# Down projection of an encoder layer: two column halves with kept operands, and seven half-block products with operands made step by step

## The chip, the cores and the metric

The kernel runs on one core of a Trainium2 chip. The metric is the device time of one execution in microseconds (us). A core has five engines that run side by side and meet through semaphores: TensorE (PE, with its weight loads listed as PEld), VectorE (DVE), ScalarE (ACT), GpSimd (POOL) and SyncE (SP), which issues nearly all DMAs here. Each engine takes its instructions in a fixed order that is laid out when the kernel is built.

## The reference

One encoder layer on 1024 tokens of width 1024, float32: a mixer, a cross attention and a gated feed-forward block, each followed by a layer norm of `alpha * h + f(h)`. The change touches the last block alone:

```
def conv_ffn(x, w_up, b_up, w_dw, b_dw, w_down, b_down):
    h = x @ w_up + b_up
    h = depthwise conv of width 3 over positions (h, w_dw) + b_dw
    g, u = jnp.split(h, 2, axis=-1)
    y = jax.nn.gelu(g, approximate=False) * u
    return y @ w_down + b_down

h = layer_norm(ALPHA * h + conv_ffn(h, ...), ln3_w, ln3_b)
```

`y` is 1024 tokens x 2816 features, `w_down` 2816 x 1024.

## The kernel before

**Arithmetic.** Float32 products are made from float16 pairs. An operand is scaled by a power of two and split (`split16`, L204 and L205): ACT writes `hi`, DVE writes `lo = scaled - hi`. `mm3` (L225 to L227) then issues three matmuls, hi x hi, hi x lo and lo x hi. The scale of an operand comes from the largest sum of absolute values of its rows (`scale_of`, L183 to L189): a small matmul `mx` spreads the maxima over the partitions and a few one-column DVE operations make the power of two.

**Up projection.** The loop `for v in range(NFF)` runs over 22 units of 128 gate and 128 value columns. It makes 2x2 blocks of each unit with seven products in place of eight (names `A11 B11` to `A22 T4`); a product is 12 matmuls of 128x512. POOL makes sums of the unit's blocks (L1505 to L1508), ACT and DVE split them two units ahead, ACT and DVE take the products out of PSUM (`take`), and `post(v)` (L1586 to L1594) runs the convolution, the GELU and the product with the value half, stores `y_d[v]` to DRAM with one DMA, and sums the absolute values of `y` for its scale. `survey_down` reads `w_down` for its scale. Unit v's last two products run in iteration v + 1.

**Down projection.** For the first 20 feature blocks the scale of `y` is taken in the last unit (`y_scale(0)`), and another for the last two blocks later (`y_scale(1)`, with `ratio` between the two). `y_pair` loads two blocks of `y` into the `ur` buffers and splits them; the 22 split blocks stay in SBUF and serve both column halves. `w_pair` loads and splits a column half of four blocks of `w_down`. `dmm` adds a list of blocks into one PSUM bank. The first column half runs over five groups of four blocks with eight token tiles in eight banks; the last unit's two remaining products stand in its first group. DVE copies the sums to `half0`. The second half goes tile by tile: POOL makes the residual `r * rw + rb` (L1795, L1796) of a tile of `h2_d`, DVE adds `half0` (L1798) and the PSUM sums (L1801, L1803), then `ln_tile` (L238 to L257) normalises the row, with one POOL operation for the power and one for the bias, and SP stores it.

**Order.** SP, POOL and the other engines take their work in the order that the builder lays out from the program's order and its own estimate of readiness. Buffers are handed on when their last reader is done: `wraw` has two, `whi` and `wlo` five each, `ur` two.

## Time and profile before

| | us |
|---|---|
| runs, median of 3 | 1548.47 (1541.97 to 1549.49) |
| the profiled execution, time | 1548.25 |
| its span, first to last instruction | 1546.5 |
| PE busy in the span | 1471.3 (95%) |
| DVE busy | 1053.5 (68%) |
| ACT busy | 811.2 (52%) |
| POOL busy | 573.3 (37%) |
| mean granted TensorE clock | 0.983 |

The profile is one execution recorded by the hardware profiler. A row of a group reads: line, engine, operation, output<-input tiles, shape, count | busy us in all, mean ns of one | idle time of the engine just before them, and what ended most of it. A row of a timeline reads: start, duration, engine, line, operation, tiles, count, and in brackets the idle time before it and what ended it; neighbours of one line are joined ("x2"), and then the duration runs over both. Matmuls overlap, so a matmul's duration (0.38) is longer than the distance between two starts.

### The profile page before, as it was taken

The page shows a single profiled execution, that of the slowest core. Times are in us where ns is not written, and L with a number is a line of the kernel's source. Part 1 is how long each engine was busy: PE and PEld are TensorE (multiplying, and loading weights), DVE is VectorE, ACT ScalarE, POOL GpSimd, SP SyncE. Part 2 cuts the span into 40 slices and gives each one's busy share as a digit, 9 for nine tenths or more (in the row PEclk, how much of TensorE's full clock was granted, in tenths as well). Part 3 has the DMA queues.
Part 4 walks back from the last instruction along what each step waited for, and adds up shares of the span by engine and source line. Part 5 has one row for each costly group of instructions (what it writes and reads, how often), then busy time and mean ns, then how long its engine had stood idle before and what let it go on. Part 6 is the DMA issues. An engine that isn't in the chain of part 4 may idle for free.

```text
span 1546.5 us, 21750 instructions
## 1 busy us (share of the span) xinstructions
PE 1471.3 (95%) x8134; PEld 877.8 (57%) x8134; DVE 1053.5 (68%) x1961; ACT 811.2 (52%) x1369; POOL 573.3 (37%) x446
## 2 busy tenths in 40 slices
PE   8899899999999899999999997999999999999997
PEld 6788787456765788874455443444444444444443
DVE  7875857535767778575357678888888777947333
ACT  5434475665553576423244676777777765722000
POOL 6243265412334766134112274444444420112252
PEclk9999999999999999999999999999999999999999
DMA  8843554314644742643001333222222433842111
GB/s 297 311 157 127 187 190 168 102 48 113 164 153 146 226 137 82 245 169 145 28 28 55 126 126 120 110 109 109 109 109 109 161 125 101 308 150 82 46 64 55
DMA packets 84896, 208.62 MB, mean 135 GB/s; under 512 B 7091, under 2 KB 36019, under 8 KB 81462
## 3 DMA queue, kind: packets, MB, share of 16 engines
q1 hardware_dynamic: 84496, 206.46, 38.3%
q8 instruction: 64, 1.05, 0.3%
q0 software_dynamic: 144, 0.49, 0.2%
q14 instruction: 42, 0.34, 0.1%
q10 hardware_dynamic: 150, 0.27, 0.0%
HBM read 158.34 MB, written 49.35 MB: 134 GB/s over the span
## 4 chain that ended last, share of the span: by engine, by line
PE 57%; DVE 21%; DMA 8%; ACT 8%; issue 4%; SPq 1%; POOL 1%; DVEq 0%; ACTq 0%; POOLq 0%
PE dn L226 5%; PE dn L227 5%; PE dn L225 5%; PE S L225 4%; PE S L227 4%; PE S L226 4%; DMA sv<-in_w_down_dram 3%; DVE cbuf L1587 3%; DVE cbuf L1588 3%; DVE wlo L205 2%; PE cl L225 2%; PE tk L225 2%; PE cl L227 2%; PE cl L226 2%; PE tk L227 2%
## 5 line engine op out<-in xcount | busy, mean ns | idle before, releaser
L1505 POOL TENSOR_TENSOR wraw<-ur 128x512 f32<-128x512 f32 x22 | 43.2, 1963 | 197.6 <-issue 189.4
L226 PE MATMUL dn<-wlo,yp 128*128 128x512 f16 x272 | 103.3, 382 | 2.7 <-DVE wlo L205 2.7
L1587 DVE SCALAR_TENSOR_TENSOR cbuf<-C,wdw,cbuf 128x1024 f32<-128x1024 f32 x44 | 79.9, 1818 | 35.7 <-ACT cbuf L1586 35.7
L227 PE MATMUL dn<-whi,yp 128*128 128x512 f16 x272 | 103.5, 382 | 0.0
L225 PE MATMUL dn<-whi,yp 128*128 128x512 f16 x272 | 102.9, 382 | 0.5 <-ACT whi L204 0.5
L226 PEld LDWEIGHTS <-whi 128*128 128x128 f16 x540 | 53.3, 99 | 61.8 <-issue 9.4
L227 PEld LDWEIGHTS <-wlo 128*128 128x128 f16 x540 | 53.4, 99 | 61.2 <-DVE wlo L205 5.3
L225 PEld LDWEIGHTS <-whi 128*128 128x128 f16 x540 | 53.2, 99 | 55.5 <-ACT whi L204 2.1
L253 ACT ACTIVATE r<-r,lnrs 128x1024 f32<-128x1024 f32 x19 | 23.6, 1243 | 114.5 <-DVE lnrs L252 114.5
L205 DVE SCALAR_TENSOR_TENSOR wlo<-wraw,us,whi 128x1024 f16<-128x1024 f32 (+1 forms) x48 | 65.5, 1381 | 23.6 <-ACT whi L204 23.3
L1588 DVE SCALAR_TENSOR_TENSOR cbuf<-C,wdw,cbuf 128x1024 f32<-128x1024 f32 x44 | 72.0, 1637 | 1.3
L243 POOL TENSOR_TENSOR lnrs<-lnrs,mhalf 128x1 f32<-128x1 f32 x32 | 18.8, 590 | 115.0 <-DVE lnrs L242 99.4
L227 PEld LDWEIGHTS <-yp 128*128 128x128 f16 x352 | 34.5, 98 | 44.9 <-issue 3.8
L1586 ACT ACTIVATE cbuf<-C,bdw,wdw 128x1024 f32<-128x1024 f32 x44 | 54.3, 1237 | 10.5 <-DVE C L1623 9.8
L225 PE MATMUL tk<-whi,Be 128*128 128x256 f16 (+1 forms) x192 | 54.8, 286 | 4.6 <-DVE stage L205 3.3
L225 PEld LDWEIGHTS <-yp 128*128 128x128 f16 x352 | 34.5, 98 | 42.6 <-issue 1.4
L226 PEld LDWEIGHTS <-yp 128*128 128x128 f16 x352 | 34.6, 98 | 41.9 <-issue 0.8
L204 ACT ACTIVATE whi<-wraw,us 128x1024 f16<-128x1024 f32 (+1 forms) x48 | 51.2, 1103 | 13.1 <-DVE us L177 11.1
L225 PE MATMUL tk<-whi,Bo 128*128 128x256 f16 (+1 forms) x192 | 52.9, 275 | 2.4 <-DVE gm L399 2.4
L226 PE MATMUL tk<-wlo,Be 128*128 128x256 f16 (+1 forms) x192 | 54.5, 285 | 0.0
L227 PE MATMUL tk<-whi,Be 128*128 128x256 f16 (+1 forms) x192 | 54.5, 284 | 0.0
L1182 ACT ACTIVATE P<-P,mn 128x256 f32<-128x256 f32 (+1 forms) x64 | 35.7, 558 | 34.0 <-DVE mn L1180 33.8
(502 smaller groups left out, 4941.4 us busy)
## 6 DMA issues: line engine op xcount, KB each, us to landing
ur<-in_w_up_dram SPq DMA_DIRECT2D x22, 1024.0 KB
sv<-in_w_down_dram SPq DMA_DIRECT2D x22, 512.0 KB
y<-cbuf SPq DMA_DIRECT2D x22, 512.0 KB
ur<-y SPq DMA_DIRECT2D x11, 1024.0 KB
wraw<-in_w_down_dram SPq DMA_DIRECT2D x22, 512.0 KB
r<-h SPq DMA_DIRECT2D x19, 512.0 KB
h<-r SPq DMA_DIRECT2D x16, 512.0 KB
wraw<-in_w_tok_dram SPq DMA_DIRECT2D x10, 512.0 KB
```

The lines of the kernel that those rows point to most:

```text
L204: A.activation(hi, src, AF.Copy, scale=s)
L205: return V.scalar_tensor_tensor(lo, src, s, hi, op0=OP.mult, op1=OP.subtract)
L225: T.matmul(ps, lh, rh, start=first, stop=False, skip_group_check=skip)
L226: T.matmul(ps, lh, rl, start=False, stop=False, skip_group_check=skip)
L227: return T.matmul(ps, ll, rh, start=False, stop=last, skip_group_check=skip)
L243: G.tensor_tensor(rs[:, 0:1], rs[:, 0:1], mhalf[:, 0:1], OP.pow)
L253: A.activation(r, r, AF.Identity, scale=rs[:, 0:1], bias=rs[:, 1:2])
L1182: A.activation(P[:, :nk], P[:, :nk], AF.Exp, scale=-1.0, bias=mn[:, 0:1], accum_out=mn[:, 1:2])
L1505: G.tensor_tensor(S1, A21, A22, OP.add)
L1586: A.activation(c, C[:, 1:SEQ + 1], AF.Identity, scale=wdw[:, 1, j:j + 1], bias=bdw[:, j:j + 1])
L1587: V.scalar_tensor_tensor(c, C[:, 0:SEQ], wdw[:, 0, j:j + 1], c, op0=OP.mult, op1=OP.add)
L1588: V.scalar_tensor_tensor(c, C[:, 2:SEQ + 2], wdw[:, 2, j:j + 1], c, op0=OP.mult, op1=OP.add)
```

## The change

The down projection is cut into 2x2 blocks: features 0 to 1407 and 1408 to 2815 (11 blocks of 128 each, `NH`), output columns 0 to 511 and 512 to 1023, and even and odd token tiles. It is computed as seven products (`order`), each over 11 steps and four token tiles in four PSUM banks. A step is one feature block: one operand of 128x512 from `y` and one of 128x512 from `w_down`.

- `load_step` loads the parts of a step, `prep_step` makes its sums and differences on POOL and DVE and splits them, `step` issues its 12 matmuls (three for each of four tiles). `ahead` keeps splits 6 steps (first product) or 10 steps ahead of the matmuls and loads 10 or 13 ahead. Thirteen buffers hold split operands, five hold loaded parts; the blocks A and B of the first product and the sums S and T stay in pages.
- The eleven steps of the first product are loaded in the last unit but one and the first six split in the last unit, with a scale from the first half of `y`; all other products use a scale from all of `y`, known after the last `post`. `ratio` brings the first product to it.
- `y_d[v]` is stored with two DMAs, even and odd token tiles apart, in runs of 512 bytes.
- `residual` computes `h2 * rw + rb` on POOL in every second unit and stores it in `res_d`; at the end `rows` loads it and ACT multiplies it by the scale.
- After each product its four banks are added to `M`, `U` or the rows, on ACT, DVE and POOL. The even tiles are normalised after the fifth product, with the weight multiplied on POOL (`weng`); the odd ones in the last product, which runs two tiles over all steps, then the third, then the fourth.

```diff
+            def residual(tt):
...
+                S.dma_start(r, h2_d[tt * 128:(tt + 1) * 128, :])
+                G.tensor_tensor(r, r, rw, OP.mult)
+                G.tensor_tensor(r, r, rb, OP.add)
+                S.dma_start(res_d[tt * 128:(tt + 1) * 128, :], r)
+            order = ("A11 B11", "S1 T1", "S2 T2", "A12 B21", "S4 B22", "S3 T3", "A22 T4")
+            steps = [(n, j) for n in order for j in range(NH)]
+            def load_step(i):
...
+                if i % 5 < 2:
+                    t = wp.tile([128, WP], F32, name="wraw", tag="wraw", bufs=2)[:, :1024]
                 else:
+                    t = page["pool"].tile([128, 1024], F32, name="tm", tag="tm", bufs=3)
...
+                S.dma_start(t0, y_part(h, a, j))
+                if n == "S1 T1":
+                    S.dma_start(page["S"][j], y_part(0, 1, j))
+                    S.dma_start(page["T"][j], w_part(0, 1, j))
+                elif n != "S4 B22":
+                    S.dma_start(t1, w_part(n != "S3 T3", n == "S3 T3", j))
+            def prep_step(i):
...
+                elif n == "S1 T1":
+                    G.tensor_tensor(page["S"][j], page["S"][j], y, OP.add)
+                    V.tensor_tensor(page["T"][j], page["T"][j], B_, OP.subtract)
+                    y, w = page["S"][j], page["T"][j]
+                elif n == "S2 T2":
+                    y, w = page["S"][j], page["T"][j]
+                    G.tensor_tensor(y, y, A_, OP.subtract)
+                    V.tensor_tensor(w, B_, w, OP.subtract)
+                elif n == "S4 B22":
+                    G.tensor_tensor(y, y, page["S"][j], OP.subtract)
+                    w = B_
+                elif n == "S3 T3":
+                    G.tensor_tensor(y, A_, y, OP.subtract)
+                    V.tensor_tensor(w, B_, w, OP.subtract)
+                elif n == "A22 T4":
+                    G.tensor_tensor(w, w, page["T"][j], OP.subtract)
...
+                split16(o[0], o[1], y, sc_y[i >= NH])
+                split16(o[2], o[3], w, sd)
+            def step(ps, i, qs):
+                j = i % NH
+                yh, yl, wh, wl = ops[i]
+                for q in qs:
+                    c = slice(q * 128, q * 128 + 128)
+                    mm3(ps[q], yh[:, c], yl[:, c], wh, wl, j == 0, j == NH - 1)
...
+            for m in range(7):
...
+                if m == 6:
+                    for j in range(NH):
+                        ahead(i0 + j, 10, 13)
+                        step(ps, i0 + j, (0, 1))
+                    for q in range(4):
+                        if q > 1:
+                            for j in range(NH):
+                                step(ps, i0 + j, (q,))
+                        r0, r1, r = odd[q]
+                        add(V, r0, ps[q])
+                        finish(r, 2 * q + 1, late=q == 3)
+                    break
+                for j in range(4 if m == 0 else 0, NH):
+                    ahead(i0 + j, 10 if m else 6, 13 if m else 10)
+                    step(ps, i0 + j, range(4))
+                    if (m, j) == (1, 0):
+                        even = rows("X2l", 0)
+                    if (m, j) == (5, 3):
+                        odd = rows("X1h", 1)
+                        for q in range(4):
+                            add(G, odd[q][1], U[q])
+                for q in range(4):
+                    if m == 0:
+                        A.activation(M[q], ps[q], AF.Copy, scale=ratio)
+                    if m == 1:
+                        A.activation(U[q], ps[q], AF.Copy)
+                        add(G, even[q][0], M[q])
+                    if m == 2:
+                        add(V, M[q], ps[q])
+                        add(G, U[q], M[q])
+                        add(G, even[q][1], U[q])
+                    if m == 3:
+                        add(V, even[q][0], ps[q])
+                    if m == 4:
+                        add(V, even[q][1], ps[q])
+                        finish(even[q][2], 2 * q, weng=G)
+                    if m == 5:
+                        add(V, M[q], ps[q])
+                        add(V, odd[q][1], ps[q])
+                        add(G, odd[q][0], M[q])
```

More of the change, by code (lines that the diff above doesn't have):

```diff
@@ L1667, in dmm @@
-            def dmm(ps, tt, c, fs, first, last):
-                t0 = slice(tt * 128, tt * 128 + 128)
-                for f in fs:
-                    wh, wl = wdn[c, f // 4]
-                    mm3(ps, ys[f][0][:, t0], ys[f][1][:, t0], wh[:, f % 4, :], wl[:, f % 4, :],
-                        first and f == fs[0], last and f == fs[-1])
-            sy = {}
-            def y_scale(g):
-                sy[g] = scale_of(ysum[:, :NG] if g == 0 else ysum[:, NG:], 14)
+            rw, rb = vec(2, "ln2_w"), wk.tile([128, D], F32, name="rb")
@@ new lines, in prep_step @@
+            def prep_step(i):
+                n, j = steps[i]
+                A_, B_ = page["A"][j], page["B"][j]
+                y, w = temps.pop(i, (None, None))
+                if n == "A11 B11":
+                    y, w = A_, B_
+                elif n == "S1 T1":
[14 more added lines that the diff above has]
+                    G.tensor_tensor(w, w, page["T"][j], OP.subtract)
+                k = i % 13 if i >= NH else i % 2 * 5
+                if k < 10:
+                    t = wp.tile([128, 2048], F16, name=("whi", "wlo")[k // 5], tag=("whi", "wlo")[k // 5], bufs=5)
+                else:
+                    t = page["pool"].tile([128, 2048], F16, name="op", tag="op", bufs=3)
+                o = ops[i] = [t[:, q * 512:q * 512 + 512] for q in range(4)]
+                split16(o[0], o[1], y, sc_y[i >= NH])
+                split16(o[2], o[3], w, sd)
@@ new lines, in ahead @@
+            def ahead(i, preps, loads):
+                while at[0] < len(steps) and (at[0] <= i + loads or at[1] + 1 > at[0]):
+                    load_step(at[0])
+                    at[0] += 1
+                while at[1] < len(steps) and at[1] <= i + preps:
+                    prep_step(at[1])
+                    at[1] += 1
+            def step(ps, i, qs):
[4 more added lines that the diff above has]
+                    mm3(ps[q], yh[:, c], yl[:, c], wh, wl, j == 0, j == NH - 1)
@@ L1706, in encoder @@
                 if v == NFF - 1:
[L1707 removed]
+                    for i in range(2, 4):
+                        prep_step(i)
                 if v > 0:
```

212 lines of the change are left out of this document (96 added, 116 removed).

## The prediction

> **What bounds the kernel now.** I read the page first, then the stage table over the end of the run, then the chain of waits, then the timelines of single engines around the clashes. In the stage table the columns after the stretch are its length and the busy time and count of PE, PEld, DVE, ACT and POOL, then the granted clock, the DMA share and GB/s.
>
> ```profile
> span 1546.5 us, 21750 instructions
> PE 1471.3 (95%) x8134; PEld 877.8 (57%) x8134; DVE 1053.5 (68%) x1961; ACT 811.2 (52%) x1369; POOL 573.3 (37%) x446
> ```
> ```profile
> 940.00:960.00 20.00, 14.68 (x60) 6.18 (x58) 17.36 (x18) 14.24 (x17) 7.83 (x4) 0.85 0.27 105
> 1000.00:1060.00 60.00, 60.00 (x282) 27.29 (x281) 50.30 (x54) 45.13 (x52) 27.98 (x15) 1.00 0.34 130
> 1300.00:1330.00 30.00, 26.73 (x116) 11.65 (x115) 26.89 (x24) 21.60 (x22) 0.00 (x0) 0.94 0.80 275
> 1360.00:1390.00 30.00, 30.00 (x141) 13.58 (x139) 9.29 (x8) 5.74 (x5) 0.00 (x0) 1.00 0.48 166
> ```
>
> The up projection (1000 to 1060) and the down projection (1360 to 1390) keep PE full. In the down projection DVE and POOL have much idle time; between 940 and 960 and at 1300 PE starves. The PE timeline and the end of the chain of waits give the edges of the stage that changes:
>
> ```profile
> 1294.83 0.38 PE L225 MATMUL z<-TX1h,whi 128*128 128x512 f16 x1
> 1299.79 0.38 PE L227 MATMUL z<-TX1l,wlo 128*128 128x512 f16 x1
> 1304.90 0.38 PE L226 MATMUL dn<-wlo,yp 128*128 128x512 f16 x1 [2.73 <-DVE wlo L205]
> ```
> ```profile
> 1538.56 0.23 PE dn L227
> 1538.81 0.70 DVE wraw L1803
> ```
>
> The first two rows are the ends of 24 matmuls in a row: 4.96 / 23 = 0.2157 us each. The last up product in the main loop ends at 1300.0 (call it T); the first `dn` work then waits for its operands. The last matmul ends at 1538.8, so the stage takes T + 238.8. After it come 7.7 us of tail, which the change keeps.
>
> **PE's share of the change.** Before: 22 blocks x 8 token tiles x 2 column halves x 3 = 1056 matmuls. After: 7 products x 11 steps x 4 tiles x 3 = 924. One step is 12 x 0.2157 = 2.59 us, a product 28.5, all seven 199.3; the 24 matmuls left of the last up unit take 5.2. With nothing late PE would end at T + 204.5, 34.3 us earlier, and the scales, which are now known one unit earlier, also take away the wait after T. The start of the stage is probably that good: the first six operand pairs are 12 `lo` operations, about 8 us of DVE in the last unit, where units are no longer prepared.
>
> **What the operands cost.** Before, an operand was made once and used for many products. After, each of 66 later steps (products 2 to 7) makes two fresh operands of 128x512: ACT writes `hi`, DVE writes `lo`; 33 steps also subtract on DVE, and 55 add or subtract on POOL. No row has DVE's or ACT's split at 512, so I go by nearby rows.
>
> ```profile
> L205 DVE SCALAR_TENSOR_TENSOR wlo<-wraw,us,whi 128x1024 f16<-128x1024 f32 x15 | 18.6, 1279 | 0.0
> L205 DVE SCALAR_TENSOR_TENSOR unitYh<-ur,us,unitYh 128x1536 f16<-128x1536 f32 x4 | 7.3, 1819 | 7.4 <-ACT unitYh L204 7.4
> L204 ACT ACTIVATE whi<-wraw,us 128x1024 f16<-128x1024 f32 x14 | 15.2, 1134 | 0.0
> L1803 DVE TENSOR_TENSOR r<-r,dn 128x512 f32<-128x512 f32 x4 | 2.8, 688 | 23.0 <-PE dn L227 23.0
> L238 DVE BATCH_NORM_STATS2 lnst<-r 128x6 f32<-128x512 f32 x8 | 5.5, 688 | 0.1
> ```
> ```profile
> 1255.03 0.74 DVE L1619 SCALAR_TENSOR_TENSOR C<-z,us,C 128x512 f32<-128x512 f32 x1
> 1255.69 0.74 DVE L1613 SCALAR_TENSOR_TENSOR C<-z,us,C 128x512 f32<-128x512 f32 x1
> ```
>
> `lo`: 1.82 - 1.28 = 0.54 us per 512 columns, so 0.74 alone, and back to back one per 0.66 (the two starts). A DVE add or subtract: one per about 0.62. ACT is below 0.75 each, under 1.5 us of 2.59 per step, so ACT is no bound. DVE by itself takes 2 x 0.66 + 0.62 = 1.94 per step: it would fit.
>
> It doesn't stay by itself. These are POOL alone, then POOL and DVE together, in the two engines' timelines:
>
> ```profile
> 1117.89 1.27 POOL L1508 TENSOR_TENSOR wraw<-ur,wraw 128x512 f32<-128x512 f32 x1
> 1454.03 2.35 POOL L1795 TENSOR_TENSOR r<-r,vec 128x1024 f32<-128x1024 f32 x1 [6.66 <-DMA r<-h]
> ```
> ```profile
> 1111.19 2.19 POOL L1505 TENSOR_TENSOR wraw<-ur 128x512 f32<-128x512 f32 x1 [10.58 <-issue]
> 1113.35 2.25 POOL L1507 TENSOR_TENSOR wraw<-ur 128x512 f32<-128x512 f32 x1
> 1115.56 2.25 POOL L1506 TENSOR_TENSOR wraw<-wraw,ur 128x512 f32<-128x512 f32 x1
> 1346.19 6.61 POOL L1795 TENSOR_TENSOR r<-r,vec 128x1024 f32<-128x1024 f32 x2 [95.95 <-DMA r<-h]
> 1352.76 6.63 POOL L1796 TENSOR_TENSOR r<-r,vec 128x1024 f32<-128x1024 f32 x2
> ```
> ```profile
> 1112.17 2.30 DVE L1587 SCALAR_TENSOR_TENSOR cbuf<-C,wdw,cbuf 128x1024 f32<-128x1024 f32 x1
> 1350.57 6.61 DVE L205 SCALAR_TENSOR_TENSOR wlo<-wraw,sc,whi 128x1024 f16<-128x1024 f32 x2
> 1418.24 0.74 DVE L1777 SCALAR_TENSOR_TENSOR half<-dn,sc,half 128x512 f32<-128x512 f32 x1
> ```
>
> While POOL runs 128x1024, a DVE `lo` of 1024 takes 3.3 us (6.61 / 2) and so does POOL's add: they take turns. One turn of both is 3.3, against 1.2 for DVE alone, so DVE loses 2.1 per POOL operation of 1024, and 2.21 - 1.2 = 1.0 per one of 512 (POOL's starts are 2.21 apart). DVE's work on PSUM isn't held up: L1777 keeps 0.74 beside POOL's 2.36 us add that starts at 1418.28. Before, this clash touched a few rows; after, nearly every step has one.
>
> The page "SBUF — State Buffer" of the Trainium skill (section "SBUF: two separate sides") says that GpSimd and a DVE operation with two SBUF inputs hold their common port pair exclusively, for a whole instruction each. The turns above agree. Were it only a sharing of bandwidth, POOL could lie beside DVE and PE might end at T + 204.5; by the rule the floor worked out below, T + 226, can't be beaten.
>
> **The sum for DVE**, from the moment the common scale is known until the last operand. That scale now needs the last `post`: 10.4 us of the first four steps + 5.2 + a take of 0.74, then L1586, two STT, GELU, product and sum at 1.0 to 1.3 each for one half with the other half's STT between, about 11, and 1 for the scale: T + 28.
> - own work: 132 `lo` x 0.66 = 87.1; 33 subtractions x 0.62 = 20.5; 12 PSUM adds x 0.66 = 7.9; statistics of four even tiles, 1.9 each = 7.5. Sum 123.
> - POOL in the way: 55 operand operations + 16 adds at the ends of products = 71 x 1.0; 8 of 1024 in the even tiles' layer norm x 2.1. Sum 87.8, of which about 10 fall beside the 15.4 us of PSUM adds and statistics: 78.
> - less 5 for the sums of three steps that can be done before the scale: 196.
>
> The last operand is ready at T + 224, where PE wanted it at T + 189. After it PE has one step of two tiles and two tiles of 11 steps: 72 matmuls, 15.5. End T + 239.5, against T + 238.8: **PE's 34 us are given back**, nearly all in the last three products, since products 2 and 3 need 32 us each for PE's 28.5, products 4 and 5 win that back (14 and 26), and then the layer norm of the even tiles lies ahead of the last operands on POOL's queue.
>
> Bounds. Floor: if every gap is filled, the two engines' turns alone are 165 x 0.58 (1.1 per 1024, halved, plus a little) + 71 x 1.13 + 8 x 2.2 = 193.5; five steps' sums done early take 8.6 off: 185 + 26 + 15.5 = T + 226.5, 12 faster. Ceiling: nothing of POOL's 98 hidden, 123 + 98 + 30 + 15.5 = T + 266, 27 slower.
>
> **Waits added.** DVE's L252 waits for POOL's power, with the next operands queued behind it:
>
> ```profile
> L252 DVE TENSOR_SCALAR lnrs<-lnmv,lnrs 128x1 f32<-128x1 f32 x7 | 1.5, 212 | 12.8 <-POOL lnrs L243 12.7
> ```
>
> Four waits of 12.7 / 4 = 3.2 us stood there at no cost; now four stand in DVE's path, 0 to 13 us. I take 4, since other operands are put between. On SP the step loads (132 of 256 KB from product 2 on, 44 in product 2 alone) pass one queue, in which the stores of even tiles wait for POOL; loads run 13 steps ahead, so I cost it at nothing.
>
> ```profile
> 1.26 0.42 SPq L576 DMA_DIRECT2D memraw<-in_memT_dram  x1
> 1.73 0.44 SPq L566 DMA_DIRECT2D wr<-in_w_xk_dram  x1
> 1316.81 1.74 SPq L1662 DMA_DIRECT2D wraw<-in_w_down_dram  x2
> ```
> ```profile
> GB/s 426 401 426 418 393 426 410 418 442 410 385 389 397 389 385 279 168 16 0 49 41 270 418 418 418 434 90 49 139 377 401 418 393 377 377 410 402 401 389 373
> ```
>
> At 0.47 us apart, 44 issues take 21 us; at the 1.2 of the last SP row, 53, and product 2 would be 13 late: that is in the upper end. The bytes of product 2, 11.5 MB at about 400 GB/s (stretch 1325 to 1345), take 29. The page "SBUF — State Buffer" (section "A bandwidth-pool intuition that's wrong") gives 358 GB/s for HBM to core; by that they would take 32, still no more than DVE needs there. The row, 400 and more, decides.
>
> **In the up projection** the residual adds 16 POOL operations of 1024 in units 2 to 16, its loads and stores, and two DVE operations (2 us) in unit 0, near the stretch 940 to 960 where PE already starves. DVE has 9.7 of 60 us free at 1000 to 1060 (3 per unit); two POOL operations per two units take up to 4.2 of 6. Bounds 0 and 10 (2 + half a us each); I take 3. `y` goes out in two stores of 512-byte runs; DMA is 0.34 busy there, so nothing. What is removed with it, POOL's 16 operations and loads at the end, was beside PE and saves nothing there.
>
> **Forecast.** 1548.25 (profiled execution: span 1546.5 plus 1.75) + 0.7 + 4 + 3 = 1556. The median of the runs, 1548.47, is the same within 0.3.
>
> **Rivals.**
> 1. PE stays the bound, or nearly: POOL's layer norm slips behind the last operands (16.8 less) and the clashes fall beside other DVE work. For: the order of a queue is laid out at build time, and in the up projection L1587 is stretched only in part of its runs. Against: the two-turn sum of 193.5 in PE's 161 us (T + 28 to T + 189). Full cover gives 1514, the slipped layer norm 1539: 1514 to 1540.
> 2. Slower by much: the layer norm of the even tiles sits on POOL and makes DVE wait with operands behind it. Price: L252's 13 instead of 4, plus nothing of POOL hidden there (+10), or SP's 1.2 spacing (+13): 1567 to 1590. It decides once DVE has no lead left at product 5's end. Page "TensorE: Matmul & The Clock Gate" of the Trainium skill (Part 1) says that an idle window of about 3.4 us halves PE's clock; the row 940 to 960, with 5.3 us idle and clock 0.85, agrees, and by that a long gap would cost another 2 us.
> 3. The gain is swallowed exactly: turns without gaps, 1536 to 1545.
>
> **Chances.** Forecast, 1545 to 1567, 0.50, half of it on each side of 1556; rival 1 0.22; rival 2 0.18; rival 3 0.10, under half of it faster. A measurement tells 0.5% (7.7 us) from no change: faster 0.26, same 0.31, slower 0.43. The range leaves out rival 1's lower half and rival 2's last third: 1528 to 1583; the likeliest case's own is 1545 to 1567.
>
> **What would show it.** Right: PE idle about 30 us in products 5 to 7, ended by DVE `lo` or ACT `hi`; DVE and POOL together near full from T + 28; `lo` rows of 512 at 0.74 mixed with 1.7 to 1.9 beside POOL; the wait after T gone. Wrong: PE full to the end (rival 1; then the turns weren't the bound), or a PE gap in product 2 released by DMA (SP's spacing), or an up projection longer by over 6 us. The forecast falls if POOL's operations mostly run while DVE waits for something else.

## The result: 1590 us, slower by 2.8%

The changed kernel takes 1590.17 us (median of 5 runs, 1585.76 to 1594.57). The kernel before took 1545.89 us beside it (5 runs, 1541.97 to 1549.49). The ratio is 1.028, with a 95% interval of 1.0249 to 1.031. The forecast was 1556 with a range up to 1583, so the time lies outside the range, on the slower side.

The profiled execution of the changed kernel took 1585.76 us. The first two lines of its page:

```profile
span 1584.0 us, 22134 instructions
...
PE 1461.7 (92%) x8002; PEld 871.3 (55%) x8002; DVE 1172.3 (74%) x2082; ACT 875.7 (55%) x1495; POOL 714.7 (45%) x525
```

The span is 37.5 us longer than before's 1546.5, with 132 matmuls fewer (8002 for 8134). To see where the 37.5 us lie, the run is cut at the same two points as in the prediction: T, the end of the last up product in the main loop, and the last matmul. The PE timeline of the changed kernel:

```profile
1304.86 0.38 PE L226 MATMUL dn<-whi 128*128 128x512 f16 x1
...
1320.83 0.38 PE L228 MATMUL dn<-whi 128*128 128x512 f16 x1
...
1331.19 0.38 PE L228 MATMUL z<-TX1l,wlo 128*128 128x512 f16 x1
...
1572.34 0.38 PE L228 MATMUL dn<-op 128*128 128x512 f16 x1
```

The last `z` of the main loop ends at 1331.4, but 27 matmuls of the down projection (5.8 us; the first two rows are the first and the last of them) had already been pulled in ahead of it, in three runs of 7, 8 and 12. They belong to the later stage, so T is counted as 1325.6 here, against 1300.0 before. The last matmul ends at 1572.7.

| part of the span | before | after | difference | forecast |
|---|---|---|---|---|
| start to T | 1300.0 | 1325.6 | +25.6 | +3 |
| T to the end of the last matmul | 238.8 | 247.1 | +8.3 | +4.7 |
| after the last matmul | 7.7 | 11.3 | +3.6 | 0 |
| span | 1546.5 | 1584.0 | +37.5 | +7.7 |

The stage that was rewritten came out 3.6 us above the forecast, and the tail after it another 3.6. The main loss lies in the up projection, where only the residual, the split store of `y` and the first loads and splits of the new stage were added. One stretch of both kernels in the stage table (columns as in the prediction), before and then after:

```profile
860.00:1300.00 440.00, 420.67 (x1942) 189.81 (x1940) 346.44 (x416) 316.38 (x377) 174.27 (x102) 0.98 0.31 114
```
```profile
860.00:1300.00 440.00, 398.13 (x1809) 177.45 (x1808) 341.11 (x400) 301.64 (x361) 220.16 (x118) 0.98 0.39 134
```

PE got through 133 matmuls fewer in the same 440 us. At 0.2157 us each that is 28.7 us. Up to 860 the changed kernel had issued 15 more than the kernel before (5127 for 5112, by the same view), so at 1300 it is 118 behind, 25.5 us: the whole of T's delay. POOL has 16 operations more (118 for 102) and 46 us more of busy time. DVE is idle for 99 us in this stretch and still seems to have room. This count of matmuls between 860 and 1300 is used below for every run.

The stage rows of the changed kernel that answer to those quoted before:

```profile
940.00:960.00 20.00, 14.20 (x60) 5.93 (x59) 19.91 (x14) 11.16 (x14) 17.77 (x8) 0.93 0.53 184
1000.00:1060.00 60.00, 51.06 (x227) 22.08 (x226) 48.48 (x49) 36.94 (x44) 34.83 (x16) 0.97 0.36 123
...
1360.00:1390.00 30.00, 21.47 (x80) 8.86 (x81) 28.83 (x30) 26.20 (x41) 24.49 (x16) 0.83 0.71 250
1390.00:1420.00 30.00, 25.07 (x104) 10.58 (x102) 30.00 (x34) 15.54 (x25) 12.56 (x8) 0.89 0.00 1
1420.00:1510.00 90.00, 90.00 (x419) 40.83 (x417) 84.02 (x86) 44.25 (x63) 56.56 (x36) 1.00 0.53 169
1510.00:1540.00 30.00, 24.72 (x108) 10.62 (x106) 29.53 (x39) 16.32 (x22) 23.98 (x16) 0.94 0.50 154
1540.00:1584.00 44.00, 24.11 (x89) 9.57 (x88) 34.94 (x45) 4.34 (x4) 30.71 (x18) 0.77 0.23 96
```

Between 1000 and 1060, where PE was full before (282 matmuls), it now issues 227. In the down projection DVE is full (28.83 and 30.00 of 30) while PE has 80 and 104 matmuls in 30 us where 139 would fit: 20 us are lost at the start of product 2, the wait for the common scale with them. Products 3 to 6 (1420 to 1510) run full. Product 7 loses another 20: 197 matmuls from 1510 to the last one's end at 1572.7, where 290 would fit.

The timeline of ACT, DVE, POOL and PE in the changed kernel at those two places:

```profile
1354.10 1.06 ACT L1592 ACTIVATE cbuf<-cbuf 128x1024 f32<-128x1024 f32 x1 [6.61 <-DVE cbuf L1589]
...
1359.63 0.69 DVE L1704 TENSOR_TENSOR pgX2h<-ur,pgX2h 128x512 f32<-128x512 f32 x1 [5.56 <-DMA ur<-in_w_down_dram]
1360.24 1.22 DVE L1593 TENSOR_TENSOR cbuf<-cbuf 128x1024 f32<-128x1024 f32 x1
...
1391.95 1.75 DVE L206 SCALAR_TENSOR_TENSOR op<-pgX1l,sc,op 128x512 f16<-128x512 f32 x1
1393.12 5.05 POOL L1846 TENSOR_TENSOR rows<-rows,half 128x512 f32<-128x512 f32 x3
...
1399.30 0.74 DVE L206 SCALAR_TENSOR_TENSOR op<-pgX1l,sc,op 128x512 f16<-128x512 f32 x1
...
1400.76 1.46 PE L228 MATMUL dn<-wlo 128*128 128x512 f16 x3 [4.93 <-DVE wlo L206]
...
1532.09 13.22 DVE L206 SCALAR_TENSOR_TENSOR wlo<-tm,sc,wlo 128x512 f16<-128x512 f32 x6
...
1533.12 2.79 POOL L257 TENSOR_TENSOR rows<-rows,lw 128x1024 f32<-128x1024 f32 x1
...
1545.22 9.00 DVE L206 SCALAR_TENSOR_TENSOR op<-wraw,sc,op 128x512 f16<-128x512 f32 x4
...
1547.47 5.54 POOL L258 TENSOR_TENSOR rows<-rows,pgX2h 128x1024 f32<-128x1024 f32 x2
1550.86 0.59 PE L227 MATMUL dn<-op 128*128 128x512 f16 x1 [4.01 <-DVE op L206]
...
1554.28 0.58 PE L227 MATMUL dn<-op 128*128 128x512 f16 x1 [0.70 <-DVE op L206]
```

A `lo` of 512 takes 0.74 alone and 1.75 beside a POOL operation of 512; beside POOL's layer norm (1024) and its operand sums (512) six of them take 13.22, 2.2 each. From 1359 on PE's waits end with a `lo`, but for two: 3.57 us for the common scale and 1.76 for ACT's first `hi` after it.

The first three rows show why the scale is late. GELU of the last `post` (L1592) is done at 1355.16, but its product on DVE (L1593) starts only at 1360.24: a difference for product 3 (L1704) stands ahead of it on DVE's queue and waits 5.56 us for its load of `w_down`. SP had issued that load late, after 3.9 us of waiting for a buffer that POOL had to hand back. So 5 us of the scale's delay come from a load; what they cost in the end was not tried.

The residual's POOL operations in the up projection, as the view of the tile `res` lists them (count: least/median/most in ns, first and last start):

```profile
L1647 POOL TENSOR_TENSOR res<-res,vec x8: 2338/2838/3982, 913.1 to 1022.6; 128x1024 f32<-128x1024 f32 x8
L1648 POOL TENSOR_TENSOR res<-res,rb x8: 3211/3222/3350, 918.1 to 1025.0; 128x1024 f32<-128x1024 f32 x8
```

Written into every second unit, they all stand between 913 and 1028 us: the builder took them as early as their loads allowed.

### The profile page after: what moved, and what is told of

It is laid out like the page before. It is cut to its first block, busy times and chain, and to the rows that moved or that the text cites. A ratio compares the mean times of both kernels' runs of the same rounds, so it can differ in the third digit from the quotient of the medians.

```text
span 1584.0 us, 22134 instructions
## 1 busy us (share of the span) xinstructions
PE 1461.7 (92%) x8002; PEld 871.3 (55%) x8002; DVE 1172.3 (74%) x2082; ACT 875.7 (55%) x1495; POOL 714.7 (45%) x525
## 4 chain that ended last, share of the span: by engine, by line
PE 41%; DVE 22%; DMA 13%; ACT 10%; issue 6%; POOL 6%; SPq 1%; DVEq 0%; POOLq 0%; ACTq 0%
PE S L226 4%; PE S L228 4%; PE S L227 4%; DMA sv<-in_w_down_dram 4%; DVE cbuf L1588 3%; DVE wlo L206 3%; DVE cbuf L1589 3%; PE cl L226 2%; PE cl L227 2%; PE cl L228 2%; PE dn L228 2%; ACT whi L205 2%; ACT cbuf L1587 1%; PE dn L226 1%; PE dn L227 1%
## 5 line engine op out<-in xcount | busy, mean ns | idle before, releaser
L1588 DVE SCALAR_TENSOR_TENSOR cbuf<-C,wdw,cbuf 128x1024 f32<-128x1024 f32 x44 | 70.0, 1596 | 60.6 <-ACT cbuf L1587 60.4
L227 PEld LDWEIGHTS <-whi 128*128 128x128 f16 x664 | 65.5, 99 | 89.6 <-issue 24.0
L228 PEld LDWEIGHTS <-wlo 128*128 128x128 f16 x660 | 65.0, 99 | 89.2 <-issue 13.5
L226 PEld LDWEIGHTS <-whi 128*128 128x128 f16 x664 | 65.5, 99 | 71.3 <-ACT whi L205 2.9
L1589 DVE SCALAR_TENSOR_TENSOR cbuf<-C,wdw,cbuf 128x1024 f32<-128x1024 f32 x44 | 76.3, 1737 | 0.6
L227 PE MATMUL dn<-wlo 128*128 128x512 f16 x120 | 46.7, 389 | 9.2 <-DVE wlo L206 9.2
L226 PE MATMUL tk<-whi,Bo 128*128 128x256 f16 (+1 forms) x192 | 52.8, 275 | 0.9 <-DVE gm L400 0.9
L1183 ACT ACTIVATE P<-P,mn 128x256 f32<-128x256 f32 (+1 forms) x64 | 35.7, 558 | 32.2 <-DVE mn L1181 31.9
L1592 ACT ACTIVATE cbuf<-cbuf 128x1024 f32<-128x1024 f32 x22 | 23.2, 1056 | 53.6 <-DVE cbuf L1589 53.5
L227 PE MATMUL tk<-wlo,Bo 128*128 128x256 f16 (+1 forms) x192 | 52.7, 274 | 0.0
L1428 POOL TENSOR_TENSOR r<-r,vec 128x1024 f32<-128x1024 f32 x6 | 14.1, 2350 | 85.4 <-PE tp L1262 85.4
L228 PE MATMUL tk<-whi,Bo 128*128 128x256 f16 (+1 forms) x192 | 52.6, 274 | 0.0
L228 PE MATMUL dn<-wlo 128*128 128x512 f16 x120 | 47.1, 397 | 4.9 <-DVE wlo L206 4.9
L227 PE MATMUL dn<-whi 128*128 128x512 f16 x124 | 48.5, 391 | 2.9 <-DVE whi L206 2.9
```

The costliest lines, as they stand in the source:

```text
L226: T.matmul(ps, lh, rh, start=first, stop=False, skip_group_check=skip)
L227: T.matmul(ps, lh, rl, start=False, stop=False, skip_group_check=skip)
L228: return T.matmul(ps, ll, rh, start=False, stop=last, skip_group_check=skip)
L1183: A.activation(P[:, :nk], P[:, :nk], AF.Exp, scale=-1.0, bias=mn[:, 0:1], accum_out=mn[:, 1:2])
L1588: V.scalar_tensor_tensor(c, C[:, 0:SEQ], wdw[:, 0, j:j + 1], c, op0=OP.mult, op1=OP.add)
L1589: V.scalar_tensor_tensor(c, C[:, 2:SEQ + 2], wdw[:, 2, j:j + 1], c, op0=OP.mult, op1=OP.add)
```

## Experiments

The loss could come from the residual or, against the table, from a side effect of the new down projection on the stage ahead of it. Within the residual it could be its loads and stores, the bunching of its POOL operations, the amount of POOL work wherever it stands, or the length of a single POOL operation. Last come the versions that move POOL's work to DVE. Medians and ratios are against runs of the kernel before on the same chip.

| run | median us | ratio, 95% interval | matmuls 860 to 1300 |
|---|---|---|---|
| before | | | 1942 |
| changed kernel | 1590.17 | 1.028 (1.0249 to 1.031) | 1809 |
| e1 before + residual | 1569.89 | 1.0159 (1.0134 to 1.0184) | 1807 |
| e2 residual spaced out | 1589.25 | 1.0284 (1.026 to 1.0308) | 1810 |
| e3 operand sums on DVE | 1580.74 | 1.0227 (1.0201 to 1.0253) | 1797 |
| e4 before + split store of y | 1546.78 | 1.0008 (0.9997 to 1.0019) | 1940 |
| e5 residual's POOL operations left out | 1568.6 | 1.0147 (1.0127 to 1.0168) | 1909 |
| e6 residual's POOL operations halved | 1589.22 | 1.0286 (1.0268 to 1.0305) | 1813 |
| e8 e3 + even layer norm on DVE | 1578.46 | 1.0213 (1.0198 to 1.0228) | 1800 |
| e9 e8 + residual on DVE | 1551.03 | 1.0027 (1.001 to 1.0044) | 1898 |
| e10 e9 + adds and odd layer norm on DVE | 1545.32 | 0.9993 (0.9978 to 1.0008) | 1899 |
| e11 e10 + residual spaced out | 1549.44 | 1.0017 (1.0005 to 1.003) | 1884 |
| e12 residual left out altogether | 1559.52 | 1.008 (1.0056 to 1.0104) | 1934 |
| e13 e9 + adds on DVE | 1548.0 | 1.0006 (0.9992 to 1.002) | 1896 |
| e14 e13 + odd tiles in turn | 1544.55 | 0.9991 (0.9981 to 1.0001) | 1898 |
| e15 e10 + odd tiles in turn | 1543.67 | 0.9984 (0.9974 to 0.9993) | 1901 |

### The residual alone, and the store of y alone

e1 adds the residual's code of the change to the kernel before, which doesn't read its result; e4 adds the split store of `y` (and reads its columns accordingly).

```diff
 e1, in the loop over the units of before.py:
+                if v % 2 == 0 and v < 2 * NT + 2:
+                    residual(v // 2 - 1)
 e4, in post(v) of before.py:
-                S.dma_start(y_d[v], cg)
+                for a in range(2):
+                    S.dma_start(y_d[v, :, a * 512:a * 512 + 512]..., cg...[:, :, a])
```

> The kernel before, with the residual of the changed kernel added in the up projection and stored, and not used: the down projection stays as it was. The changed kernel's POOL timeline has all sixteen operations of 1024 of the residual between 905 and 1028 us, not one pair per two units. Theory A (that bunching takes DVE's and POOL's turns from the units, and the residual is what the up projection lost): slower by 18 to 27 us, near 1569, with PE gaps between 920 and 1060 and none after. Rival B (the two-part store of y or another order of the units costs it): within 5 us of before, near 1549.

> The kernel before, with y stored as in the changed kernel, by two DMAs in runs of 512 bytes, and the token tiles taken from their new places. Theory A: within 3 us of before, since the DMAs there are busy a third of the time. Rival B: slower by 5 us or more, with ACT or DVE waiting for the survey's loads behind it.

The residual alone costs 24.1 us (1569.89 against 1545.80), as theory A had it, and the count of matmuls falls by 135, as in the changed kernel. So the loss in the up projection comes from it and not from the new stage. The split store costs nothing that can be measured.

### What of the residual costs: its transfers, its place, its size

e5 keeps the loads and stores and leaves the two POOL operations out; e12 leaves out everything and reads `h2_d` in its place; e2 holds each load until the unit's own load and each pair of POOL operations until POOL's last sum of that unit; e6 cuts each POOL operation in two of 512 columns.

```diff
 e5:
-                G.tensor_tensor(r, r, rw, OP.mult)
-                G.tensor_tensor(r, r, rb, OP.add)
 e12:
-                    residual(v // 2 - 1)
-                    S.dma_start(t[:, q], res_d[tt * 128:(tt + 1) * 128, :])
+                    S.dma_start(t[:, q], h2_d[tt * 128:(tt + 1) * 128, :])
 e2:
+                with tc.issue_after(units.g.ins):
+                    G.tensor_tensor(r, r, rw, OP.mult)
+                    G.tensor_tensor(r, r, rb, OP.add)
 e6:
+                for c in (slice(0, 512), slice(512, D)):
+                    G.tensor_tensor(r[:, c], r[:, c], rw[:, c], OP.mult)
+                    G.tensor_tensor(r[:, c], r[:, c], rb[:, c], OP.add)
```

> The changed kernel, with the residual's loads held behind the load of the unit's weights and its POOL operations behind the unit's last sum on POOL, so that a pair stands in every second unit. Theory A (the bunching costs): 18 to 25 us less than the changed kernel, near 1568, PE full from about 970. Rival C (the amount of POOL work costs, wherever it stands): within 6 us of the changed kernel, near 1588. Rival B: no change.

> The changed kernel without the residual's two POOL operations (the rows are loaded and stored as they are, so weight, bias and b_down are left out of the residual); loads, stores and buffers stay. Between 860 and 1300 us the changed kernel loses 29 us more of PE than the kernel before, and spacing the pairs did not change that. Theory F (POOL's operations themselves, by taking turns from DVE, on whose next operation PE waits): 24 to 29 us less than the changed kernel, near 1563. Rival G (the loads and stores on SP, or the buffers): within 6 us of it, near 1587.

> The changed kernel with the residual's POOL operations as four of 512 columns in place of two of 1024. Theory F1 (the amount of turns counts): within 5 us of the changed kernel, near 1590. Rival F2 (one long turn of 2.2 us is what PE's slack can't take): 8 to 20 us less, near 1576.

> The changed kernel with no residual in the up projection; the rows are loaded from h2 as they are, so weight, bias and b_down are left out. It shows the down projection's part of the change alone. Without the POOL operations, but with loads and stores, PE's losses from 860 to 1300 came to 39.2 us against 31.5 of before. If loads and stores cost those 8, they fall to 32 and the time to about 1558; if the builder's order of the units costs them, they stay near 39 and the time near 1567. Either way the down projection alone is not faster than before: 10 to 20 us slower, since its operands come late in products 2 and 7.

The stretch 860 to 1300 of e5, then of e12:

```profile
860.00:1300.00 440.00, 414.33 (x1909) 186.61 (x1907) 340.30 (x423) 312.68 (x382) 148.75 (x102) 0.99 0.41 142
```
```profile
860.00:1300.00 440.00, 418.64 (x1934) 189.54 (x1933) 336.31 (x423) 314.66 (x385) 153.12 (x102) 0.99 0.36 123
```

Without the POOL operations 100 matmuls come back (21.6 us), and the median falls by the same 21.6 (1590.17 to 1568.6). Without the transfers too, another 25 (5.4 us; median 9.1). The rest against before, 8 matmuls, is 1.7 us. The residual as a whole costs 30.7 us (1590.17 to 1559.52). Counted as above, T is 1325.6 in the changed kernel, 1303.2 in e5 and 1298.1 in e12: without the residual the up projection is no later than before. What is left, the new down projection, is 13.7 us slower than the old one.

Spacing did not help: e2 has the same count and the same time. So bunching, which I had taken for the cause after seeing the POOL rows above, is out. Halving did not help either, so the amount of POOL work counts, not the length of one operation. Nor is it that the units' sums on POOL come later behind the residual: in e2 the pairs stand behind the unit's last sum, and the loss is the same. e2 shows how a pair costs, since its pairs stand alone. The timeline of e2 around one of them, all engines:

```profile
1130.20 2.36 POOL L1649 TENSOR_TENSOR res<-res,vec 128x1024 f32<-128x1024 f32 x1 [0.39 <-DMA res<-h]
...
1131.15 2.50 DVE L1588 SCALAR_TENSOR_TENSOR cbuf<-C,wdw,cbuf 128x1024 f32<-128x1024 f32 x1 [5.60 <-ACT cbuf L1587]
...
1132.64 3.21 POOL L1650 TENSOR_TENSOR res<-res,rb 128x1024 f32<-128x1024 f32 x1
...
1133.68 3.25 DVE L1589 SCALAR_TENSOR_TENSOR cbuf<-C,wdw,cbuf 128x1024 f32<-128x1024 f32 x1
...
1134.62 0.38 PE L228 MATMUL z<-Bh,unitYh 128*128 128x512 f16 x1
...
1136.86 0.74 DVE L1626 SCALAR_TENSOR_TENSOR C<-z,us,C 128x512 f32<-128x512 f32 x1
1137.52 0.14 DVE L1473 CAST am<-l 128x1 bf16<-128x1 f32 x1
...
1137.65 0.38 PE L226 MATMUL z<-Bh,unitA 128*128 128x512 f16 x1 [2.65 <-DVE am L1473]
...
1138.14 0.63 PE L228 MATMUL z<-Bh,unitA 128*128 128x512 f16 x1
```

DVE idles 5.60 us and then the two convolution steps of `post` arrive, 1.28 us each when alone (e2's next L1588, at 1138.91). Beside the pair they take 2.50 and 3.25: 3.2 us lost. Behind them on DVE's queue stand the take of a product out of its PSUM bank (L1626) and the small cast `am`. PE is empty for 2.65 us. The profile puts the end of its wait down to `am`, though the matmul does not read it and the take ended only 0.06 us earlier; either way both stretched steps lie ahead. The free time of DVE was there, but *ahead* of the two steps, where it waited for ACT; behind them there was none.

The wait is not the whole price. After it eight matmuls take over 0.5 us in place of 0.38 (last row) and start 0.43 apart, at a granted clock of 0.54 from 1137.7 to 1141.3: another 1.7 us. e2 has six waits of this kind, 2.6 to 4.4 us long and 18.5 in all, each followed by eight to eleven such slow matmuls. Over 860 to 1300, PE's waits add up to 36.5 us in e2 and 25.5 in e5, and 68 matmuls are slow against 24. The difference, 11 us of waiting and about 9 of slow pace, accounts for nearly all of the 21 us that e2 loses against e5 (99 matmuls).

In the changed kernel, where the pairs follow one another, the last link is mostly another one. PE's waits (41.5 us in all, 42 slow matmuls) end with `am` for 3.0 us only, and for 26.0 with ACT's takes of products (L1614 and L1620). The longest of them, in the timeline of the changed kernel:

```profile
957.12 2.28 DVE L1589 SCALAR_TENSOR_TENSOR cbuf<-C,wdw,cbuf 128x1024 f32<-128x1024 f32 x1
959.43 1.06 ACT L1592 ACTIVATE cbuf<-cbuf 128x1024 f32<-128x1024 f32 x1 [8.14 <-DVE cbuf L1589]
960.39 0.76 ACT L1614 ACTIVATE C<-z,bup,us 128x512 f32<-128x512 f32 x1
961.21 0.58 PE L226 MATMUL z<-TX1h,whi 128*128 128x512 f16 x1 [6.41 <-ACT C L1614]
```

ACT's GELU waits for a convolution step that takes 2.28 beside POOL, the take stands behind the GELU on ACT's queue, and PE waits for the take. The stretched DVE step is the same, with ACT in between. Only this one wait was followed back.

### Operand sums and layer norm of even tiles on DVE

e3 makes all operand sums on DVE in place of POOL; e8 does the even tiles' layer norm on DVE too, in the fused form that the last tile uses.

```diff
 e3, all of prep_step (here one of five):
-                    G.tensor_tensor(page["S"][j], page["S"][j], y, OP.add)
+                    V.tensor_tensor(page["S"][j], page["S"][j], y, OP.add)
 e8, besides:
-                        finish(even[q][2], 2 * q, weng=G)
+                        ln_tile(even[q][2], lw, lb, small, late=True, eps=ep)
+                        S.dma_start(out[2 * q * 128:2 * q * 128 + 128, :], even[q][2])
```

> The changed kernel, with all sums and differences of the down projection's operands on DVE, none on POOL. Theory D (DVE and POOL taking turns is what makes operands late in products 2 and 7): 55 operations of 0.62 us more for DVE, 55 turns of 1.0 us less, so 10 to 20 us less, near 1575. Rival E (DVE's own work and the waits between engines bound those products, POOL is beside them): 10 to 34 us more, near 1612.

> The run with all operand sums on DVE, and besides the even tiles' layer norm in the two fused DVE operations of the last tile's form, with no POOL operation of 1024 and no ACT step. Theory D (turns): the sixteen DVE operations of 512-equivalent cost about 10 us, eight turns of 2.1 go, and L253's waits: 6 to 12 us less than with the sums alone, near 1571, PE gaps after 1520 under 4 us. Rival E: the same or more, 1581 to 1590.

e3 gives DVE 55 operations more and is 9.4 us faster. The same group of `lo` operations, by groups of instructions, in the changed kernel, in e3 and in e15 (below), where POOL has nothing left but the powers:

```profile
L206 DVE SCALAR_TENSOR_TENSOR wlo<-tm,sc,wlo 128x512 f16<-128x512 f32 x19 | 25.8, 1404 | 0.0
```
```profile
L206 DVE SCALAR_TENSOR_TENSOR wlo<-tm,sc,wlo 128x512 f16<-128x512 f32 x19 | 19.6, 1053 | 0.0
```
```profile
L206 DVE SCALAR_TENSOR_TENSOR wlo<-tm,sc,wlo 128x512 f16<-128x512 f32 x19 | 14.0, 767 | 0.0
```

One and the same instruction takes 1404, 1053 and 767 ns on average, as POOL's work beside it goes. That is the turn-taking of the prediction, and rival E of e3 (10 to 34 us more) is out. e8 gained only 2.3 us on e3, less than theory D's 6 to 12. That is a net figure: DVE takes over the work, about 10 us by the estimate above, so it does not say what the layer norm costs on POOL.

### Everything on DVE

e9 puts the residual's two operations on DVE as well; e10 also the adds after the products and the odd tiles' layer norm; e13 the adds alone; e11 is e10 with the residual's loads spaced out.

```diff
 e9, besides e8:
-                G.tensor_tensor(r, r, rw, OP.mult)
-                G.tensor_tensor(r, r, rb, OP.add)
+                V.tensor_tensor(r, r, rw, OP.mult)
+                V.tensor_tensor(r, r, rb, OP.add)
 e13, besides e9 (all twenty, with four inside product 6; e10 also sets late=True below):
-                            add(G, ...)
+                            add(V, ...)
                         finish(r, 2 * q + 1, late=q == 3)
 e11, besides e10:
+                with tc.issue_after(loaded.ins):
                     S.dma_start(r, h2_d[tt * 128:(tt + 1) * 128, :])
```

> The same as the run with sums and even layer norm on DVE, and the residual's multiplication and addition on DVE too, none on POOL. Theory F (turns of 2.2 us on POOL cost the up projection 29): DVE pays 2.4 us per pair itself, 8 pairs, in place of two turns, so 8 to 16 us less than that run, near 1560. Rival H (what counts is any delay of DVE's order, and its own operations delay it as much): within 5 us of it.

> The run with everything of the residual, the sums and the even layer norm on DVE, and besides the sixteen adds after the products and the odd tiles' layer norm (the last tile's fused form) on DVE: POOL keeps the power alone. Theory D (turns): sixteen operations of 0.62 in place of turns of 1.0, three turns of 2.1 gone, three times 1.2 more: 4 to 9 us less, near 1545, as a tie with the kernel before or just below. Rival E: DVE is now full by itself, 0 to 6 us more.

> The same with the residual's loads held behind the load of the unit's weights, so that a pair of DVE operations stands in every second unit. Where the residual's own work is short, its place should matter: the gaps of 4 and 5 us near 955 and 998 go, 4 to 8 us less than without, near 1540. If the amount alone counts, as with POOL: within 2 us.

> The run with residual, sums, even layer norm and the adds after products on DVE, but the odd tiles' layer norm shared by ACT, DVE and POOL as in the changed kernel. With the odd tiles on DVE too, PE was done at 1526.6 and the tail after it took 19 us in place of 7.7, because DVE had four tiles to normalise one after another. Theory: the tail goes back to 8 to 12 us with PE's end where it was, 5 to 10 us less, near 1538, below the kernel before. Rival: the turns of POOL's bias adds come back and hold up the last operands, within 3 us of 1545.

e9 gains 27.4 us on e8, far more than expected. The stretch 860 to 1300 of e9, and its `res` tile:

```profile
860.00:1300.00 440.00, 415.17 (x1898) 186.06 (x1897) 372.27 (x436) 316.12 (x380) 181.17 (x102) 0.98 0.41 142
```
```profile
L1647 DVE TENSOR_TENSOR res<-res,vec x8: 1214/1226/2293, 914.0 to 1008.2; 128x1024 f32<-128x1024 f32 x8
```

The same 16 operations give DVE about 20 us more to do and cost PE 11 matmuls (2.4 us) against e5, which has the transfers alone; on POOL they cost 100. On DVE an operation takes 1.2 us. That it also stands where the queue has time, while on POOL it takes hold of DVE in the middle of the chain that PE waits for, fits these counts, but was not followed operation by operation.

e10 came where theory D had it (1545.32 for 1545). e13 did not: its tail was to fall to 8 to 12 us and is the longest. Both tie with the kernel before, although their last matmul comes 12 and 13 us earlier than before's. e13's timeline at the end, and its last matmul:

```profile
1522.95 1.33 DVE L1846 TENSOR_TENSOR rows<-rows,dn 128x512 f32<-128x512 f32 x2 [5.51 <-PE dn L228]
...
1525.34 0.38 PE L228 MATMUL dn<-op 128*128 128x512 f16 x1
...
1533.38 4.50 DVE L257 TENSOR_TENSOR rows<-rows,lw 128x1024 f32<-128x1024 f32 x2
...
1538.26 5.08 POOL L258 TENSOR_TENSOR rows<-rows,pgX2h 128x1024 f32<-128x1024 f32 x2
```

DVE runs empty for 5.51 us, then all odd tiles come ready at once: their four adds stand between 1522.95 and 1527.9, since the builder had pulled the third and fourth tiles' matmuls forward. From the end of the last matmul to the end of the span (1548.3) there are 22.6 us in e13 and 19.1 in e10, against 7.7 before. Spacing the loads (e11) was to gain 4 to 8 us on e10 and made it 4.1 us slower.

### Odd tiles in turn

e14 (from e13) and e15 (from e10) hold the third tile's matmuls behind those of the first two, and the fourth's behind the third's.

```diff
+                            with tc.issue_after(mm.ins):
                                 for j in range(NH):
-                                    step(ps, i0 + j, (q,))
+                                    mm = step(ps, i0 + j, (q,))
```

> The kernel of e13 (operand sums, even tiles' layer norm, residual and the adds after the products on DVE; odd tiles' layer norm shared with POOL), and the last product's matmuls of tile pair q=2 are held behind those of q=0 and q=1, those of q=3 behind q=2's. Theory G: in e13 the last matmul came 13 us earlier than before and the end did not, because the builder had pulled q=2's and q=3's matmuls into PE's waits, so that all four odd tiles came ready within 4 us and their layer norms stood in one queue; held, they come ready about 7 us apart, PE waits more in the last product (last matmul 1529 to 1534 instead of 1525) but the tail falls from 23 to 8 to 11 us: 1537 to 1543. Rival H: the tail is DVE's and POOL's amount of work that is left by then, wherever it stands; then the time stays within 2 us of e13's 1548.

> The same hold in the kernel of e10, whose odd tiles' layer norm is on DVE alone (1545.3 us, tail 19.5). Theory G: tail 9 to 12, 1535 to 1541, and a shade better than e14, since the last layer norms take no turns between DVE and POOL. Rival H: within 2 us of e10's 1545.

The tail fell as the first theory said, from 22.6 to 9.0 us in e14 (start of the last matmul 1538.56, span 1547.9) and from 19.1 to 7.9 in e15 (1527.73, 1536.0). The times did not follow: by the medians e14 is 3.4 us faster than e13, between theory G and rival H, and e15 1.7 faster than e10, which rival H allows (2 us). The spans of single executions mislead here: the profiled one of e15 is the fastest of its twelve (1537.76 us), and at 860, ahead of everything that differs, it had issued 33 matmuls (7 us) more than e10's. Counted from the start of the common scale (L190), the last matmul ends after 181 us in e13 and e10, after 192 in e14 and 190 in e15, and the span ends after 203.8 and 200.4, 201.2 and 198.2. So PE waits longer in place of the tail. The stage table of e14, and one of e15's `dn` groups:

```profile
1420.00:1510.00 90.00, 88.61 (x411) 40.06 (x410) 90.00 (x145) 43.32 (x61) 11.65 (x4) 1.00 0.57 184
```
```profile
L227 PE MATMUL dn<-op 128*128 128x512 f16 x64 | 26.3, 410 | 5.9 <-DVE op L206 5.9
```

DVE is busy for 90.00 of 90 us (89.31 in e15). With POOL's turns gone, DVE's own work sets the end, and the order mostly decides whether PE waits before it or the tail after it. e15 is the best version found: 0.9984 (0.9974 to 0.9993) of the kernel before, 2 to 3 us faster.

## Why the prediction was wrong

**The step that failed is the term for the up projection:** "Bounds 0 and 10 (2 + half a us each); I take 3". It measured 25.6. The argument was that DVE has "9.7 of 60 us free" and that two POOL operations per two units "take up to 4.2 of 6". The 4.2 was near (3.2 per pair in e2's rows). Idle time was the wrong thing to set against it: a row of before, not looked at then, shows where it lies (groups of DVE's instructions, 860 to 1300, idle time before them at the end):

```profile
L1587 DVE SCALAR_TENSOR_TENSOR cbuf<-C,wdw,cbuf 128x1024 f32<-128x1024 f32 x41 | 76.1, 1857 | 35.7 <-ACT cbuf L1586 35.7
```

Over a third of DVE's idle time (35.7 of 93.6) is a wait for ACT directly ahead of the convolution steps, which are the ones that POOL then stretches and behind which the steps wait that let PE go on. The upper bound should have been the full price: eight pairs at 4.2 is 34, not 10. With the 5 to 9 us of transfers that e5 and e12 show, which the prediction did not price, a bound of 40 would have held the time. The clash itself was in the prediction; it was applied to the down projection and let off in the stage beside it.

**The operands, right in kind, and in the sum partly by luck.** Turns of 1.7 to 1.9 were expected beside POOL; 1.75 was measured. The wait after T is gone (PE is busy for 30.00 and 29.42 of 30 us from 1300 and from 1330). The last operand was forecast for T + 228, waits for POOL's power included (T + 224 and 4); the `lo` that ends at 1554.22 puts it at T + 228.6. But two errors of about 10 us cancel in it: the common scale was ready at T + 39 in place of T + 28 (L178 ends at 1364.67), and from there to the last operand it took 190 us in place of 200. After it PE needed 18.5 us for the forecast 15.5, since 14 matmuls follow the last wait at half pace (granted clock 0.50 from 1554.3 to 1560). That puts the last matmul at T + 247.1 in place of T + 243.5. PE's 34 us were given back. In e10 and e13, without POOL's turns, it ends at T + 216: 23 us of the gain in PE's work then show, and go to a later T and to the tail.

**Where PE waits, half wrong.** Products 5 to 7 were named; the waits lie at product 2 (20 us) and product 7 (20 us). The late scale let product 2 begin without any lead, with DVE full. The chain on DVE sets the end either way, which is why the sum held although the place did not.

**The waits for POOL's power** were taken at 4 us in DVE's path. They add up to 4.1 us (four waits of L253 for POOL), but that is chance: only 0.44 lies ahead of the last operand, and 2.78 ends at 1573.13, when the last matmul is done. **SP's spacing** (rival 2) did not come as priced, 13 us late in product 2: no wait of PE ends with a load. But a late load is in it by way of DVE, 5.56 us ahead of the scale. The "about 400 GB/s" for the loads was the rate of the full slices; the whole stretch 1325 to 1345 moved 331. (The step loads from product 2 on are 121, not 132; no term rests on it.) **Two stores of `y`:** nothing, as taken (e4). **The tail** was to be kept at 7.7 and grew by 3.6; its rows in the changed kernel:

```profile
1574.66 1.23 DVE L257 TENSOR_TENSOR rows<-rows,lw 128x1024 f32<-128x1024 f32 x1 [1.31 <-ACT rows L254]
1575.80 0.68 DVE L1846 TENSOR_TENSOR rows<-rows,dn 128x512 f32<-128x512 f32 x1
```

The last tile's add could start at 1572.7, but stands behind the third tile's layer norm on DVE until 1575.80.

**Rival 2** gave 1567 to 1590, near the time, by another mechanism: layer norm and SP in the last products. The layer norm on POOL is there (2.2 us per `lo` beside it, and product 7 loses 20 us), but the stage as a whole came out 8.3 us longer than before, and 25.6 of the 37.5 lie ahead of it. That the time came near that range is not its doing.

**The Trainium skill**, page "SBUF — State Buffer", section "SBUF: two separate sides", has GpSimd and DVE hold their port pair for a whole instruction each. The traces agree: a `lo` of 0.74 us takes 1.75 beside a POOL operation of its size. That halved POOL operations (e6) cost as much as whole ones, 1589.22 against 1590.17, fits it too, since the port is held for the same time in sum. The floor that the prediction drew from the turns, T + 226.5 with POOL at work, was not beaten by the changed kernel.

**What stays open.** How the residual's transfers cost 5 to 9 us was not looked for further. The largest single gap left in e10 and e13 is a wait of 7 to 8 us for ACT's first operands at the start of product 2. ACT waits there for the scale: in e10 its first DVE step (L185) starts at 1350.53, 4.8 us after the reduction ahead of it (L190 at 1345.72), because operand sums stand between them on DVE's queue, two of them waiting for loads (1.09 and 0.44). Whether another order would close the gap was not tried.

## What to carry to other kernels

Before work is put on POOL beside a stage that PE fills, look at where DVE's idle time lies: a wait ahead of a DVE step that PE's next work depends on is no room. Where POOL operations met such a step here, PE waited nearly as long as the step was stretched (2.65 us for 3.2 in the pair shown) and then ran slowly for a while; spacing them out or halving them changed nothing. The same work on DVE itself can be nearly free (16 operations: 2.4 us on DVE, 21.6 on POOL). When PE's work is cut by making more operands, add up DVE's work to the end first; where that sum was the longer one here, a better order mostly moved the wait.

## What the runs showed of the hardware that was not expected

- An operation of 128x1024 that DVE does in 1.2 us costs PE 1.35 us when it runs on POOL (21.6 / 16): more than DVE would need to do it itself.
- After each of the six waits of 2.6 to 4.4 us in e2, PE issued eight to eleven matmuls at half pace, 0.43 us apart in place of 0.2157. Five of the six are shorter than the 3.4 us named under rival 2. Slow matmuls of this kind make up about 9 of the 21 us that the residual's POOL operations cost there.
- Stores of `y` in runs of 512 bytes, two for one, cost nothing at a DMA share of about 0.3: 1.0008 (0.9997 to 1.0019).
- 132 matmuls fewer, 28.5 us of PE time, were worth 0.2% at best (e15).
